# Second block's mixers: w_in in unsplit 32-bit matmuls, and split buffers in six tiles instead of three

## The chip, the cores and the metric

The kernel runs on one core of a Trainium2 chip. Its engines are named in the profile as PE (TensorE matmuls), PEld (TensorE weight loads), DVE (VectorE), ACT (ScalarE), POOL (GpSimd) and SP (SyncE, which here only issues DMAs). The metric is the device time of one launch in microseconds; the median of three runs before the change is 2834.43 us (2833.59 to 2838.01).

## The reference, cut to what matters

A first block of two layers (attention mixers, a dense feed-forward and a mixture of experts) is followed by a second block of two layers. The change lies in the second block. A token block is x of 256 x 1024; all arithmetic is float32.

```
for l in range(2):
    h = rmsnorm(x, norm_mix_g[l])
    proj = h @ w_in[l]                       # 1024 x 4896
    qa, ka, va, qd, kd, vd, beta, decay, z, gates = split(proj)
    y_attn = grid_attention(rope(qa), rope(ka), va) @ w_o_attn[l]
    qkv = silu(conv5(concat(qd, kd, vd)))
    o = bidir_gated_deltanet(l2norm(qd), l2norm(kd), vd, beta, g)
    y_dn = (rmsnorm(o) * silu(z)) @ w_o_dn[l]
    x = x + (sigmoid(gates0) * y_attn + sigmoid(gates1) * y_dn) @ w_out[l]
    h = rmsnorm(x, norm_ffn_g[l])
    u = conv3(h @ w_up[l])                   # 1024 x 5632
    x = x + (silu(u_gate) * u_val) @ w_down[l]   # 2816 x 1024
```

The delta rule is computed in chunks of 64 tokens, both directions, with a triangular inverse for each chunk and head.

## The kernel before, in words

**Split products.** A float32 matmul is computed as three faster ones. A weight tile of 1024 columns is split: ACT writes the rounded part `wh` (L152), DVE or POOL subtracts it from the raw weights and writes the rest `wl` (L154). The input is split in the same way into `xTh` and `xTl` (`make_xT`, L209 and L210). A product is then wh·xh + wl·xh + wh·xl: `mm3` (L177 to L179) where the input is the stationary operand and tokens are the output's rows, and `feat_group` (L370 to L372) where the weights are stationary and features are the output's rows.

**Weights.** All weight matrices stand in one list of jobs, in order of use; a job is at most one megabyte (128 x 2048 floats) and is loaded by one DMA on SP's queue (`_dma`, L137). In the second block a job goes to one of two buffers (tag raw, RAW = 2). Jobs are cut into pieces of at most 1024 columns (`subs`), split ahead of use into three pairs of buffers (HALF = 3; `_split`, `fill`). `w()` gives the next piece to the code that multiplies. In the second block's mixer `share` is 2: every second subtraction goes to POOL; behind a `tok_parts` with `tail`, the next four go to POOL too (TURN). A load may be issued when the buffer's earlier job is one that has come into use; on the chip it waits until the last reader of that buffer has finished.

**The second block's mixer** (`mix2`), in order of its code: z and the delta rule's small inputs (`zgate(0)`, 272 columns of w_in), two groups of 256 columns of the delta rule's inputs (`dnfeat` 2 and 3, each followed by a convolution on DVE, L1172), the attention's q, k, v (512 and 256 columns, `tok_group`), `zgate(1)`, four more `dnfeat`, eight gate groups of 256 columns into `m` and `G8`, then w_o_attn, w_o_dn and `out_proj` with w_out. The delta rule (`delta`) is a generator between them: decay factors (L1406 to L1465), gram matrices and the triangular inverse on DVE (`XP`, L1580 to L1607), the last part of the inverse on PE (L1663, L1669), then 16 steps of pairs (`pair`, L1708 to L1754). Its element-wise products qk and kd run on POOL (L1622), placed behind the last split on POOL (`s.gq`). After `out_proj`, `rms_h` normalises each half of the tokens (L1122 to L1132) and transposes it on PE. Tiles named kd, qk and xv belong to the delta rule; xTl is the second half of the split input.

**The order.** Within an engine instructions run in a fixed order. That order is not the code's: a planner with a cost for each instruction places them by priority, weight splits with a high one (PRIO), and may put matmuls of later groups between the small ones of the delta rule. `behind` forbids an instruction to be placed before another one; the last gate group and w_o_attn are kept behind the delta rule's last step in this way.

Of the kernel before, what the change touches and what calls it, by code (L numbers as in the profile page):

```python
# [11 lines left out]
F32 = mybir.dt.float32  # L12
F32R = mybir.dt.float32r
# [4 lines left out]
OP = mybir.AluOpType  # L18
# [3 lines left out]
S = 256  # L22
NT = 2
KD = D // 128
# [8 lines left out]
class Net:  # L33
    def __init__(s, ctx, tc, A):
        s.tc, s.nc, s.A = tc, tc.nc, A
        s.const = ctx.enter_context(tc.tile_pool(name="const", bufs=1))
        s.wa = ctx.enter_context(tc.tile_pool(name="wa", bufs=1))
        s.pm = ctx.enter_context(tc.tile_pool(name="psum", bufs=1, space=bass.MemoryType.PSUM))
        s.sc = ctx.enter_context(tc.tile_pool(name="sc", bufs=2))
        s.n_ps = 0  # L40
        s.wx = (0, 0)
        s.share, s.turn = 0, -9
        s.st, s.hs = [None, None], [None, None]
        s.epi = []
        s.pace = None
        s.jobs = []
        s.subs, s.subj = [], []
# [3 lines left out]
        s.n_dma = s.n_split = s.n_used = s.n_raw = 0  # L51

    @contextmanager
# [19 lines left out]
    BANKS = dict(mm=2, sd=3, at=2, ex=1)  # L73
    SHARE = 2
    TURN = 4
    PRIO = 3000
    AHEAD = (7, 11)

    def add_jobs(s, jobs):
        for ap, k, n, kind in jobs:  # L80
            j = len(s.jobs)
            s.jobs.append((ap, k, n))
            if kind == "f":
# [13 lines left out]
    def feats(s, w, c0, n):  # L97
        k = w.shape[0] // 128
        v = w.rearrange("(k p) n -> p k n", p=128)
        return [(v[:, :, c0:c0 + n], k, n, "f")]  # L100

    def rows(s, w, step):
# [17 lines left out]
    def _dma(s, j, c):  # L120

        ap, k, n = s.jobs[j]
        tag = s.more(j)
        if tag:
            key, bufs, pool = tag, 1, s.const if tag in ("OA", "Wc", "xTh", "xTl") else s.reg
        elif j >= s.edge_j or s.n_ring % (s.RAW + s.wx[0]) < s.RAW:
# [12 lines left out]
        return True  # L139

    def _split(s, i):
        k0, k, n0, n = s.subs[i]
        raw = s.jobs[s.subj[i]][:, k0:k0 + k, n0:n0 + n]
        r = []
        for tag in ("wh", "wl"):
            if i >= s.edge_i or i % (s.HALF + s.wx[1]) < s.HALF:
                w = s.wa.tile([128, 1024], F32R, tag=tag, name=tag, bufs=s.HALF)
            else:
                w = s.wb.tile([128, 1040], F32R, tag=tag, name=tag, bufs=s.wx[1])[:, 8:1032]
            r.append(w[:, :k * n].rearrange("p (k n) -> p k n", k=k))  # L150
        with s.tc.high_priority(offset=s.PRIO):
            s.nc.scalar.copy(r[0], raw)  # L152
            eng = s.nc.gpsimd if 0 <= i - s.turn < s.TURN or s.share and i % s.share == 0 else s.nc.vector
            x = eng.tensor_tensor(out=r[1], in0=raw, in1=r[0].bitcast(F32), op=OP.subtract)  # L154
            if eng is s.nc.gpsimd:
                s.psub = x
        s.subs[i] = (r[0], r[1], k, n)

    def fill(s, ahead):
        last = min(s.n_used, len(s.subs) - 1)  # L160
        while s.n_dma < len(s.jobs) and s._dma(s.n_dma, s.subj[last]):
            s.n_dma += 1
        ahead = min(s.n_used + ahead, max(s.n_used + s.HALF, s.edge_i), len(s.subs))
        while s.n_split < ahead and s.subj[s.n_split] < s.n_dma:
            s._split(s.n_split)
            s.n_split += 1

    def w(s):
        s.fill(s.HALF + s.wx[1])
        r = s.subs[s.n_used]  # L170
        s.subs[s.n_used] = None
        s.n_used += 1
        return r
# [138 lines left out]
    def tok_parts(s, n, K, xch, lead=0, tail=0, tags=("mm", "mm")):  # L312
# [4 lines left out]
        pend, base = [], 0  # L317

        def run(tt, bs):
            tsl = slice(tt * 128, tt * 128 + 128)  # L320
            ends = []
            for b0, h, l, k in pend:
                for kk in range(k):
                    c = b0 + kk
                    xh, xl = xch(c)
                    for b in bs:
                        ns = slice(b * 512, min(n, b * 512 + 512))
                        ends.append(s.mm3(pss[tt][b][:, :ns.stop - ns.start], xh[:, tsl], xl[:, tsl], h[:, kk, ns],
                                      l[:, kk, ns], c == 0, c == K - 1))
            return ends[-1]  # L330

        i = 0
        if tail:
            s.turn, k = s.n_used, 0
            while k < K:
                u = s.subs[s.turn]
                k += u[1] if len(u) == 4 and isinstance(u[1], int) else u[2]
                s.turn += 1
        while base < K:
# [3 lines left out]
            i += 1  # L343
            if i < lead or base > K - tail and base < K:
                continue
# [11 lines left out]
    def tok_group(s, n, K, xh, xl, lead=0):  # L357
        return [p for _, _, p in s.tok_parts(n, K, lambda c: (xh[:, c], xl[:, c]), lead)]

    def feat_group(s, ps, xh, xl):  # L360
        mm = s.nc.tensor.matmul
        b = 0
        while b < ps.shape[1]:
            h, l, k, n = s.w()
            for j in range(n // 128):
                o = ps[:, b, :]
                sl = slice(j * 128, j * 128 + 128)
                for kk in range(k):
                    with s.paced():
# [441 lines left out]
    def moe(s, i, j, pp):  # L811
# [96 lines left out]
        for tt in range(NT):  # L908
            for n in range(2):
                s.layernorm(tt, n, gb, lambda tt, n: s.rms_h(tt, n, gain))  # L910

# [201 lines left out]

    def rms_h(s, tt, n, gain):

# [14 lines left out]
        for n in range(2):  # L1130
            ns = slice(n * 512, n * 512 + 512)
            nc.vector.scalar_tensor_tensor(h[:, ns], x(n), r, gain[:, ns], op0=OP.mult, op1=OP.mult)  # L1132
            s.make_xT(tt, h, (n,))

# [5 lines left out]
    def jobs_mix2(s, l):  # L1140
# [52 lines left out]
    def mix2(s, l):  # L1193
        nc, A = s.nc, s.A
        s.share = s.SHARE
        xh, xl = s.xTh, s.xTl
        cw = s.vec_T(A["dn_conv_w_2"][l].rearrange("k (b p) -> (k b) p", p=128), 60, "cw")
# [26 lines left out]
        def dnfeat(g):  # L1224
            ps = s.fps()
            s.feat_group(ps, xh, xl)
            u = cT[g // 4][:, 2 * g % 8:2 * g % 8 + 2, :]
# [35 lines left out]
        for g in (0, 1, 4, 5):  # L1263
            dnfeat(g)
        s.gq = s.psub
        next(dn)
# [16 lines left out]
        mT = []  # L1283
        s.share = 0
        for g in range(4):
            gs = slice(2 * g, 2 * g + 2)
# [110 lines left out]
    def delta(s, l, cT, zb, sv, hg):  # L1397
# [459 lines left out]
def program(tc, A, out):  # L1857
    with ExitStack() as ctx:
# [19 lines left out]
        with s.region("two", 0, 0, "mm"):  # L1878
# [3 lines left out]
            gain = s.rms_gain("norm_mix_g_2", 1)  # L1882
            s.ffn2(0, lambda tt, n: s.rms_h(tt, n, gain))
            s.mix2(1)
# [17 lines left out]
```

## Time and profile before

| | us |
|---|---|
| median of three runs | 2834.43 |
| profiled execution | 2838.87 |
| its span, first to last instruction | 2837.1 |
| first block | 0 to about 1827 |
| second block, layer 0: mixer, w_out and norm, feed-forward | 1827 to 2095, 2095 to 2132, 2132 to 2325 |
| second block, layer 1: mixer, w_out and norm, feed-forward | 2325 to 2607, 2607 to 2644, 2644 to 2837 |

The stretches are read from where the matmuls of each weight matrix begin in the timeline. Matmul records overlap: each has a tail of some 0.16 us behind the time in which the next one starts, so a busy PE is not a full one. The mean granted clock of TensorE over the span is 0.963.

### The profile page before, as it was taken

The page shows a single profiled execution, that of the slowest core. Times are in us where ns is not written, and L with a number is a line of the kernel's source. Part 1 is how long each engine was busy: PE and PEld are TensorE (multiplying, and loading weights), DVE is VectorE, ACT ScalarE, POOL GpSimd, SP SyncE. Part 2 cuts the span into 40 slices and gives each one's busy share as a digit, 9 for nine tenths or more (in the row PEclk, how much of TensorE's full clock was granted, in tenths as well). Part 3 has the DMA queues.
Part 4 walks back from the last instruction along what each step waited for, and adds up shares of the span by engine and source line. Part 5 has one row for each costly group of instructions (what it writes and reads, how often), then busy time and mean ns, then how long its engine had stood idle before and what let it go on. Part 6 is the DMA issues. An engine that isn't in the chain of part 4 may idle for free. (4 is left out here: it accounts for less than half of the span.)

```text
span 2837.1 us, 42537 instructions
## 1 busy us (share of the span) xinstructions
PE 2664.6 (94%) x16177; PEld 2322.2 (82%) x16177; DVE 2194.8 (77%) x3347; ACT 1723.8 (61%) x2643; POOL 513.8 (18%) x427
## 2 busy tenths in 40 slices
PE   8999999899999999999999999788989989799899
PEld 7988998798787878778788777577779977688897
DVE  6576654657788989889888998789777858977784
ACT  5464543456477778787777777565645535564553
POOL 3235000132400000000000000166520016641100
PEclk9999999999999999999999999898899999889999
DMA  7336564544779999999999998533145543213454
GB/s 216 120 120 200 179 193 158 170 127 147 243 265 362 350 346 362 343 347 359 360 340 354 353 353 290 178 107 105 38 150 167 182 149 122 90 53 120 149 181 161
DMA packets 350097, 610.39 MB, mean 215 GB/s; under 512 B 13626, under 2 KB 175752, under 8 KB 349888
## 3 DMA queue, kind: packets, MB, share of 16 engines
q1 hardware_dynamic: 347120, 601.34, 61.8%
q0 software_dynamic: 2768, 6.28, 1.0%
q8 instruction: 129, 2.11, 0.3%
q14 instruction: 80, 0.66, 0.1%
HBM read 606.56 MB, written 1.05 MB: 214 GB/s over the span
## 5 line engine op out<-in xcount | busy, mean ns | idle before, releaser
L152 ACT CAST wh<-raw 128x1024 fp32r<-128x1024 f32 (+3 forms) x1154 | 1186.7, 1038 | 705.6 <-PE mm L371 189.5
L154 DVE TENSOR_TENSOR wl<-raw,wh 128x1024 fp32r<-128x1024 f32 (+3 forms) x1031 | 1246.1, 1226 | 398.7 <-ACT wh L152 379.3
L370 PE MATMUL mm<-xTh,wh 128*128 128x256 f32 x1632 | 472.1, 289 | 5.3 <-DVE cT L1172 2.9
L372 PE MATMUL mm<-xTh,wl 128*128 128x256 f32 x1632 | 470.9, 289 | 3.4 <-DVE wl L154 1.7
L371 PE MATMUL mm<-xTl,wh 128*128 128x256 f32 x1632 | 472.8, 290 | 0.0
L154 POOL TENSOR_TENSOR wl<-raw,wh 128x1024 fp32r<-128x1024 f32 (+3 forms) x123 | 293.4, 2390 | 908.4 <-ACT wh L152 872.9
L178 PE MATMUL mm<-wl,xg 128*128 128x512 f32 x896 | 355.1, 396 | 1.6
L177 PE MATMUL mm<-wh,xg 128*128 128x512 f32 x896 | 352.8, 396 | 0.0
L179 PE MATMUL mm<-wh,xg 128*128 128x512 f32 x896 | 351.5, 392 | 0.0
L370 PEld LDWEIGHTS mm<-xTh,wh 128*128 128x128 f32 x1632 | 316.1, 194 | 11.6 <-issue 3.8
L372 PEld LDWEIGHTS mm<-xTh,wl 128*128 128x128 f32 x1632 | 316.6, 194 | 7.3 <-DVE wl L154 2.3
L371 PEld LDWEIGHTS mm<-xTl,wh 128*128 128x128 f32 x1632 | 315.0, 193 | 1.0
L178 PEld LDWEIGHTS mm<-wl,xg 128*128 128x128 f32 x896 | 168.3, 188 | 43.2 <-DVE wl L154 7.7
L177 PEld LDWEIGHTS mm<-wh,xg 128*128 128x128 f32 x896 | 168.3, 188 | 36.7
L179 PEld LDWEIGHTS mm<-wh,xg 128*128 128x128 f32 x896 | 168.4, 188 | 36.4
L178 PE MATMUL sd<-wl,ac 128*128 128x512 f32 x448 | 175.7, 392 | 0.0
L642 POOL DMA_DIRECT2D gb<-in_ln_ffn_g_dram x2 | 1.1, 564 | 963.2 <-DMA raw<-in_expert_w_dram 962.9
L179 PE MATMUL sd<-wh,ac 128*128 128x512 f32 x448 | 175.6, 392 | 0.0
L177 PE MATMUL sd<-wh,ac 128*128 128x512 f32 x448 | 143.9, 394 | 0.0
L370 PE MATMUL ex<-xTh,wh 128*128 128x256 f32 x384 | 112.1, 292 | 4.7 <-DVE cT L1172 4.7
L372 PE MATMUL ex<-xTh,wl 128*128 128x256 f32 x384 | 111.4, 290 | 1.5 <-POOL wl L154 1.5
L371 PE MATMUL ex<-xTl,wh 128*128 128x256 f32 x384 | 112.0, 292 | 0.0
(581 smaller groups left out, 4939.1 us busy)
## 6 DMA issues: line engine op xcount, KB each, us to landing
raw<-in_expert_w_dram SPq DMA_DIRECT2D x336, 1024.0 KB, 5.7
raw<-in_w_in_dram SPq DMA_DIRECT2D x74, 1024.0 KB, 5.1
raw<-in_w_up_dram SPq DMA_DIRECT2D x44, 1024.0 KB, 5.0
raw<-in_dense_w_dram SPq DMA_DIRECT2D x33, 1024.0 KB, 5.2
raw<-in_w_down_dram SPq DMA_DIRECT2D x22, 1024.0 KB, 4.9
raw<-in_w_out_dram SPq DMA_DIRECT2D x16, 1024.0 KB, 5.0
raw<-in_w_branch_diff_dram SPq DMA_DIRECT2D x8, 1024.0 KB, 4.9
raw<-in_w_ple_gate_dram SPq DMA_DIRECT2D x8, 1024.0 KB, 5.0
```

Source lines behind the costliest of these rows:

```text
L152: s.nc.scalar.copy(r[0], raw)
L154: x = eng.tensor_tensor(out=r[1], in0=raw, in1=r[0].bitcast(F32), op=OP.subtract)
L177: mm(out, lhsT=lh, rhs=rh, start=start, stop=False)
L178: mm(out, lhsT=lh, rhs=rl, start=False, stop=False)
L179: return mm(out, lhsT=ll, rhs=rh, start=False, stop=stop)
L370: mm(o, lhsT=h[:, kk, sl], rhs=xh[:, kk, :], start=kk == 0, stop=False)
L371: mm(o, lhsT=h[:, kk, sl], rhs=xl[:, kk, :], start=False, stop=False)
L372: mm(o, lhsT=l[:, kk, sl], rhs=xh[:, kk, :], start=False, stop=kk == k - 1)
L642: s.nc.gpsimd.dma_start(gb[:, 0], row_bc(s.A[nm + "_g"], i * D, D))
```

## The change

The first item is that w_in of the second block is no longer split. Its jobs get the kind "w": one piece each, raw, no cast and no subtraction. The normalised input of the mixers is kept as one float32 tile `xf` in xTh's place (`make_xf`), and products with `l is None` are one matmul of float32 operands. `dnfeat` 2 and 3 multiply the two halves of the tokens apart. Raw jobs of w_in are held until their matmuls have read them; they may use xTl's tile as a third buffer (and in layer 1, for jobs 2 and 3, kd's tile as well).

The second is that a free pair of buffers is found by use, not by index (`_slot`), and from w_o_dn to the start of the next mixer the tiles kd, qk and xv serve as three more pairs, six in all (`s.ext`). The third is that no subtraction of the second block is on POOL: `share` is no longer set in `mix2`, TURN is gone (in the first block too), and the products on POOL no longer wait behind a split.

```diff
+    def unsplit(s, jobs):
+        return [(*j[:3], "w") for j in jobs]
...
+        if j >= s.edge_j:
+            def last(key, bufs):
+                use = s.held.setdefault(key, [])
+                return use[-bufs] if len(use) >= bufs else -1
+
+            key, bufs = min([("wa", s.RAW)] + [(t, 1) for t in s.alt.get(j, ()) if s.alt_on], key=lambda k: last(*k))
+            tag, pool = {"wa": ("raw", s.wa), "xTl": ("xTl", s.const)}.get(key) or (key, s.reg)
...
+    def _slot(s, i):
+        some = [("wa", s.HALF)]
+        if s.wx[1] and i < s.edge_i:
+            some.append(("wb", s.wx[1]))
+        for key, bufs in some + [(t, 1) for t in s.ext]:
+            use = s.busy.setdefault(key, [])
+            if len(use) < bufs or use[-bufs] < s.n_used:
+                use.append(i)
+                return key
...
+        if i in s.whole:
+            s.subs[i] = (raw, None, k, n)
+            return
...
-            eng = s.nc.gpsimd if 0 <= i - s.turn < s.TURN or s.share and i % s.share == 0 else s.nc.vector
-            x = eng.tensor_tensor(out=r[1], in0=raw, in1=r[0].bitcast(F32), op=OP.subtract)
+            eng = s.nc.gpsimd if s.share and i % s.share == 0 else s.nc.vector
+            eng.tensor_tensor(out=r[1], in0=raw, in1=r[0].bitcast(F32), op=OP.subtract)
...
+        if rl is None:
+            return mm(out, lhsT=lh, rhs=rh, start=start, stop=stop)
...
+    def make_xf(s, tt, src, g):
+        if tt == 0 and g == 0:
+            s.xf = s.const.tile([128, KD, S], F32, tag="xTh", name="xf")
+        pt = s.ps([128, 4, 128], "sd")
+        for c in range(4):
+            s.tr(pt[:, c, :], src[:, (4 * g + c) * 128:(4 * g + c + 1) * 128])
+        s.nc.scalar.copy(s.xf[:, 4 * g:4 * g + 4, tt * 128:tt * 128 + 128], pt)
...
+                if l is None:
+                    for t in (slice(0, 128), slice(128, 256)) if apart else (slice(0, 256),):
+                        for kk in range(k):
+                            mm(o[:, t], lhsT=h[:, kk, sl], rhs=xh[:, kk, t], start=kk == 0, stop=kk == k - 1)
...
+        J = s.unsplit(J)
+        for i in range(len(J)):
+            s.alt[len(s.jobs) + i] = ("xTl", "kd") if l and i in (2, 3) else ("xTl",)
...
-        s.share = s.SHARE
-        xh, xl = s.xTh, s.xTl
+        s.ext = ()
+        xh, xl, s.alt_on = s.xf, None, True
...
-        s.gq = s.psub
...
         s.share = 0
+        s.ext = ("kd", "qk", "xv")
...
+        s.alt_on = False
         gain = s.rms_gain("norm_ffn_g_2", l)
...
-        def PT(**k):
-            with s.behind(s.gq):
-                nc.gpsimd.tensor_tensor(**k)
+        PT = nc.gpsimd.tensor_tensor
```

## Rows read from the trace of the kernel before

**Rows 1.** the page: busy time (share of the span) and instructions

```profile
PE 2664.6 (94%) x16177; PEld 2322.2 (82%) x16177; DVE 2194.8 (77%) x3347; ACT 1723.8 (61%) x2643; POOL 513.8 (18%) x427
```

**Rows 2.** stretches: length, busy (records) of PE, PEld, DVE, ACT, POOL, clock, DMA

```profile
1827.00:2007.00 180.00, 157.69 (x1038) 141.00 (x1036) 164.31 (x308) 103.82 (x208) 111.77 (x99) 0.90 0.33 101
1882.00:2007.00 125.00, 107.38 (x718) 95.02 (x718) 121.68 (x214) 76.75 (x155) 83.48 (x80) 0.89 0.31 94
1958.00:2007.00 49.00, 45.02 (x328) 40.97 (x326) 48.00 (x84) 30.48 (x65) 23.60 (x19) 0.93 0.29 87
2007.00:2062.00 55.00, 51.14 (x421) 40.97 (x422) 35.56 (x119) 34.45 (x112) 25.44 (x42) 0.84 0.10 31
2062.00:2095.00 33.00, 31.22 (x268) 30.40 (x267) 28.59 (x56) 14.89 (x24) 5.77 (x3) 1.00 0.46 145
```

**Rows 3.** chain of waits, 1827 to 2095, shares by line

```profile
by line: issue 7.3%; DVE wl L154 6.5%; DVE cT L1172 3.6%; DVE XP L1580 3.5%; DVE XP L1606 3.4%; DVE Ma L1534 3.3%; PE sd L1732 2.8%; PE sd L1719 2.6%; DVE rs_t L189 2.5%; DVE rs_t L190 2.4%; ACT wh L152 2.2%; PE at L1741 2.1%; PE mm L177 2.
```

**Rows 4.** PE: timeline (start, length), chain piece, source line (ns min/median/max)

```profile
1838.34 0.28 PE L370 MATMUL ex<-xTh,wh 128*128 128x256 f32 x1
1838.70 0.28 PE L370 MATMUL ex<-xTh,wh 128*128 128x256 f32 x1
1888.37 1.45 PE L1512 MATMUL sd<-rg,tri 128*128 128x512 f32 x3
L1512 PE MATMUL sd<-rg,tri x16: 590/594/1062, 1885.9 to 2393.5; 128*128 128x512 f32 x16
2097.14 0.23 PE mm L177
```

**Rows 5.** records with xTl on PE (one per product) by stretch

```profile
1827.00:2095.00 268.00, 88.32 (x288) 0.90 0.30 92
2325.00:2607.00 282.00, 90.33 (x288) 0.87 0.29 91
```

**Rows 6.** those with the tile wl: PE, PEld, DVE, POOL

```profile
1827.00:2007.00 180.00, 83.30 (x265) 54.45 (x265) 22.40 (x19) 44.86 (x18) 0.90 0.33 101
2062.00:2095.00 33.00, 22.33 (x81) 15.20 (x80) 8.54 (x7) 4.82 (x2) 1.00 0.46 145
```

**Rows 7.** DVE timeline, a step alone and steps over a POOL split

```profile
1836.78 2.36 DVE L154 TENSOR_TENSOR wl<-raw,wh 128x1024 fp32r<-128x1024 f32 x1 [1.69 <-ACT wh L152]
1840.57 0.18 DVE L1415 TENSOR_SCALAR sp<-sp 128x32 f32<-128x32 f32 x1
1841.63 2.38 DVE L1419 TENSOR_SCALAR sp<-sp 128x32 f32<-128x32 f32 x1
1979.73 1.85 DVE L1606 TENSOR_TENSOR XP<-X,XP 128x512 f32<-128x512 f32 x1
```

**Rows 8.** chain piece in which PE waits for w_out's split

```profile
2110.26 1.05 ACT wh L152
```

**Rows 9.** norm behind w_out: POOL timeline, chain pieces, like steps

```profile
2116.71 6.98 POOL L154 TENSOR_TENSOR wl<-raw,wh 128x1024 fp32r<-128x1024 f32 x3 [0.24 <-DVE X L1556]
2116.81 2.31 DVE r_y L202
2119.45 1.97 DVE r_y L202
2121.44 2.81 DVE h L1132
L1132 DVE SCALAR_TENSOR_TENSOR h<-xt,r_y,g x16: 737/749/2796, 1824.6 to 2641.6; 128x512 f32<-128x512 f32 x16
```

**Rows 10.** start of layer 1's mixer: chain pieces, source line

```profile
2324.37 1.80 DVE r2v L1127
2326.66 0.61 DVE xTl L210
L1127 DVE SCALAR_TENSOR_TENSOR r2v<-r x8: 149/160/1865, 1822.3 to 2638.6; 128x1 f32<-128x1 f32 x8
```

**Rows 11.** loads of w_in, KB each, median us to landing

```profile
raw<-in_w_in_dram SPq DMA_DIRECT2D x17, 1024.0 KB, 5.0
```

More of the change, by code (lines that the diff above doesn't have):

```diff
@@ L41, in __init__ @@
         s.wx = (0, 0)
-        s.share, s.turn = 0, -9
+        s.share = 0
         s.st, s.hs = [None, None], [None, None]
@@ L46, in __init__ @@
         s.jobs = []
-        s.subs, s.subj = [], []
+        s.subs, s.subj, s.whole, s.alt, s.alt_on = [], [], set(), {}, False
         s.edge_j = s.edge_i = s.n_ring = 0
@@ L51, in __init__ @@
         s.n_dma = s.n_split = s.n_used = s.n_raw = 0
+        s.busy, s.ext = {}, ()
     @contextmanager
@@ L73 @@
     BANKS = dict(mm=2, sd=3, at=2, ex=1)
-    SHARE = 2
-    TURN = 4
     PRIO = 3000
@@ L82, in add_jobs @@
             s.jobs.append((ap, k, n))
-            if kind == "f":
+            if kind == "w":
+                s.whole.add(len(s.subs))
+                s.subs.append((0, k, 0, n))
+            elif kind == "f":
                 c = min(n, 1024 // k)
@@ L139, in _dma, with _split @@
         return True
-    def _split(s, i):
+    def _slot(s, i):
[7 more added lines that the diff above has]
+                return key
+    def _split(s, i, slot):
         k0, k, n0, n = s.subs[i]
         raw = s.jobs[s.subj[i]][:, k0:k0 + k, n0:n0 + n]
+        if i in s.whole:
+            s.subs[i] = (raw, None, k, n)
+            return
         r = []
[L145 to L149, printed above, removed]
+        if slot in ("wa", "wb"):
+            pool, bufs = (s.wa, s.HALF) if slot == "wa" else (s.wb, s.wx[1])
+            n8 = 8 if slot == "wb" else 0
+            ws = [pool.tile([128, 1024 + 2 * n8], F32R, tag=tag, name=tag, bufs=bufs)[:, n8:n8 + 1024]
+                  for tag in ("wh", "wl")]
+        elif slot == "xv":
+            ws = [s.reg.tile([128, 1024], F32R, tag=slot, name="ww", bufs=2) for _ in range(2)]
+        else:
+            w = (s.const if slot in ("OA", "Wc") else s.reg).tile([128, 2, 1024], F32R, tag=slot, name="ww")
+            ws = [w[:, 0], w[:, 1]]
+        for w in ws:
             r.append(w[:, :k * n].rearrange("p (k n) -> p k n", k=k))
@@ L162, in fill, with w @@
             s.n_dma += 1
-        ahead = min(s.n_used + ahead, max(s.n_used + s.HALF, s.edge_i), len(s.subs))
-        while s.n_split < ahead and s.subj[s.n_split] < s.n_dma:
-            s._split(s.n_split)
-            s.n_split += 1
[L168 to L173, printed above, removed]
+        while ahead and s.n_split < len(s.subs) and s.subj[s.n_split] < s.n_dma:
+            slot = s.n_split in s.whole or s._slot(s.n_split)
+            if slot is None:
+                break
+            s._split(s.n_split, slot)
+            s.n_split += 1
+    def w(s, n=1):
+        s.fill(1)
+        r = s.subs[s.n_used:s.n_used + n]
+        s.subs[s.n_used:s.n_used + n] = [None] * n
+        s.n_used += n
+        return r if n > 1 else r[0]
     def mm3(s, out, lh, ll, rh, rl, start, stop):
         mm = s.nc.tensor.matmul
+        if rl is None:
+            return mm(out, lhsT=lh, rhs=rh, start=start, stop=stop)
         mm(out, lhsT=lh, rhs=rh, start=start, stop=False)
@@ L327, in run @@
                         ns = slice(b * 512, min(n, b * 512 + 512))
-                        ends.append(s.mm3(pss[tt][b][:, :ns.stop - ns.start], xh[:, tsl], xl[:, tsl], h[:, kk, ns],
-                                      l[:, kk, ns], c == 0, c == K - 1))
+                        ends.append(s.mm3(pss[tt][b][:, :ns.stop - ns.start], xh[:, tsl], None if l is None else xl[:, tsl],
+                                          h[:, kk, ns], None if l is None else l[:, kk, ns], c == 0, c == K - 1))
             return ends[-1]
         i = 0
[L333 to L338, printed above, removed]
         while base < K:
@@ L343, in tok_parts @@
             i += 1
-            if i < lead or base > K - tail and base < K:
+            if base < K and (i < lead or base > K - tail):
                 continue
@@ L357, in tok_group, with feat_group @@
     def tok_group(s, n, K, xh, xl, lead=0):
-        return [p for _, _, p in s.tok_parts(n, K, lambda c: (xh[:, c], xl[:, c]), lead)]
-    def feat_group(s, ps, xh, xl):
+        return [p for _, _, p in s.tok_parts(n, K, lambda c: (xh[:, c], None if xl is None else xl[:, c]), lead)]
+    def feat_group(s, ps, xh, xl, apart=False):
         mm = s.nc.tensor.matmul
@@ L909, in moe @@
             for n in range(2):
-                s.layernorm(tt, n, gb, lambda tt, n: s.rms_h(tt, n, gain))
+                s.layernorm(tt, n, gb, lambda tt, n: s.rms_h(tt, n, gain, True))
     def moe_rest(s, j, xs):
@@ L1111, in diff_attn, with rms_h @@
         s.steps.append(s.last_tr)
-    def rms_h(s, tt, n, gain):
+    def rms_h(s, tt, n, gain, full=False):
         nc = s.nc
@@ L1132, in rms_h @@
             nc.vector.scalar_tensor_tensor(h[:, ns], x(n), r, gain[:, ns], op0=OP.mult, op1=OP.mult)
-            s.make_xT(tt, h, (n,))
+            if full:
+                s.make_xf(tt, h, n)
+            else:
+                s.make_xT(tt, h, (n,))
     def rms_gain(s, nm, l):
@@ L1225, in dnfeat @@
             ps = s.fps()
-            s.feat_group(ps, xh, xl)
+            s.feat_group(ps, xh, xl, g in (2, 3))
             u = cT[g // 4][:, 2 * g % 8:2 * g % 8 + 2, :]
@@ L1882, in program @@
             gain = s.rms_gain("norm_mix_g_2", 1)
-            s.ffn2(0, lambda tt, n: s.rms_h(tt, n, gain))
+            s.ffn2(0, lambda tt, n: s.rms_h(tt, n, gain, True))
             s.mix2(1)
```

8 lines of the change are left out of this document (4 added, 4 removed).

## The prediction, made before the result was known

> **What bounds the kernel now.** I read the page's busy table first: over the whole span PE is busy 94% and DVE 77% [rows 1], so the span alone says TensorE. Then the stages of the second block, by the busy time in stretches [rows 2]. There it differs: in the mixer of layer 0, from 1882 to 2007 us, DVE is busy 121.7 of 125 us and PE 107.4; from 1827 to 2007 PE is busy 157.7 of 180 us, and as a PE record carries a modelled tail, PE is emptier than that. From 2007 to 2062 (the delta rule's 16 steps) both have air: a chain of small steps. From 2062 to 2095 PE is full (31.2 of 33). Layer 1's mixer has the same 288 products and takes 282 us where layer 0's takes 268 [rows 5]. The chain of waits agrees [rows 3]: from 1827 to 2095 its largest named parts are DVE's; the split's subtraction (L154) alone is 6.5% of 268 = 17.4 us and its cast (ACT L152) 2.2% = 5.9 us. So in the mixers the weight split stands on the path, and the reader should see that DVE is the bound there and PE not quite.
>
> **The change, part by part.**
>
> *1. PE, added.* One product of w_in was three matmuls and becomes one 32-bit matmul. Three of 256 columns take 1838.70 - 1838.34 = 0.36 us; three of 512 take 3 x 0.23 = 0.69 [rows 4]. A 32-bit call is two records (the loop at L1512 makes 8 calls in two layers, and there are 16 records); three records of 512 columns fill 1.45 us, the last one 0.59, so one takes (1.45 - 0.59)/2 = 0.43, a call 0.86, and with 256 columns half, 0.43 [rows 4]. A layer has 288 products [rows 5]: by the code 240 of 256 columns, 32 of 272, 16 of 512. Added: 240 x 0.07 + 32 x 0.08 + 16 x 0.17 = 16.8 + 2.6 + 2.7 = 22.1 us a layer, 265/288 of it (20.3) before 2007. The two groups cut into halves of 128 columns I cost at no difference; if their shorter records ran at 0.12 instead of 0.11 it would be 32 x 4 x 0.01 = 1.3 us.
> The Trainium skill (FP8 and Floating Point Precision, "TensorE Precision Notes") says that true FP32 takes four passes through the array. If each cost what a split pass costs here, a product of 256 columns would be 4 x 0.12 = 0.48 against 0.36, and a layer would gain about 35 us on PE instead of 22. The trace shows two records of double length, and this measured 0.43 is what I sum with.
>
> *2. DVE, ACT and POOL, removed.* From 1827 to 2007 there are 19 subtractions on DVE, 22.4 us, and 18 on POOL, 44.9 us [rows 6]; all are of w_in and go, with their casts on ACT (1.05 us each). The ones on POOL cost DVE as well: DVE instructions that meet one are stretched to its end. A 128x32 TENSOR_SCALAR takes 0.18 us alone and 2.38 at 1841.63, over a POOL split [rows 7]. Going through the timeline, 14 DVE instructions between 1827 and 2007 are over 0.4 us longer than their like while a POOL split runs, first at 1836.78 and last at 1979.73 [rows 7], 22.5 us in all. So DVE gets back up to 22.4 + 22.5 = 44.9 us: with its idle time as it is, a lower end of 180 - 44.9 = 135 us. What is late next is PE: its 157.7 + 20.3 = 178 us is the upper end if its present busy time were all real work. It is not: 795 of its records there are w_in's (3 x 265) at 0.12 to 0.23, about 99 us, and the other 243 of the 1038 I put at the same 0.12, 29 us, together 128, new 148, which leaves about 32 idle at 180. Between 135 and 178 I take 164, nearer to PE's row, because PE would then be at 148/164 = 90%: -16 us a layer. The casts hide inside that.
> [...]
>
> *3. After the delta rule (2062 to 2095).* Only one gate group of w_in is left (+1.1 us on PE). POOL's two splits there (4.8 us) go to DVE (+2.4), and stretch DVE no more. PE is the bound; more split buffers let it wait less. -1 us, bounds +4 and -4. In layer 1 w_in's last group sits in one of the two ring buffers (in layer 0, by the rotation of three, in xTl's place), and now holds it until its matmuls are done, so the next load (at most the 5.0 us of a full megabyte [rows 11], and then a cast of 1.05 and a subtraction of 1.2 us) starts about a group, 7 us, later, and only one group of w_o_attn, 8 products of 0.36 us, covers it: +4 us once, 0 to +6.
>
> *4. w_out and the norm behind it.* Here PE waits for one cast of w_out, 1.05 us [rows 8], and its subtraction (22.4/19 = 1.2 us as in [rows 6]); six slots instead of three let these run earlier: -2 us (0 to -2.25). Then, with PE waiting, the norm's DVE steps meet three POOL splits of w_up (6.98 us): 2.31, 1.97 and 2.81 us against 0.16, 0.16 (what a step on one column takes [rows 10]) and 0.75 alone [rows 9], 6.0 us lost on the path. These splits now go to DVE at 1.2 us each, at worst all in the same place: 3.6. Between -6 and -2.4 I take -3.
>
> *5. Start of a mixer.* The transposed input is one copy instead of cast and subtraction; the subtraction (0.61 us [rows 10]) goes, and so does the POOL split that made a 128x1 step take 1.80 us there [rows 10] (median 0.16). -2 us (0 to -3). The loads: unsplit buffers are held until the matmuls end, three of them in rotation; a megabyte takes 5.0 us [rows 11] and a group on PE 16 x 0.43 = 6.9, so the load of the group after next is hidden; if only two rotated, each group would show up to 5.0 us.
>
> *6. First block.* A few splits behind its out-projections move from POOL to DVE as well; the same trade as in 4, three places, 0 (-3 to +3). w_up and w_down are bound by PE; six slots do nothing for them.
>
> Sum: a layer -16 - 1 - 2 - 3 - 2 = -24; two layers -48, +4 for layer 1: **-44 us**. The profiled execution took 2838.87 us around its span of 2837.1; the median of the runs is 2834.43. From that median: **2790 us**.
>
> **Rivals.**
>
> *A. DVE is all of it.* The stage falls to about 154 instead of 164, with gates moved into the delta rule's gaps. For: DVE's 121.7 of 125. Against: PE would need 148/154 = 96% of the stage. 10 us more in each layer: 2770.
>
> *B. PE takes the bound.* The mixer up to 2007 stays at about 178 and only parts 3 to 6 remain: 2 x (-2 - 8) + 4 = -16: 2818. For: 157.7 + 20.3. Against: the tails in that number.
>
> *C. Slower: gates pushed behind the delta rule.* PE takes its work in a planned order, and w_in's gates fill its gaps. Where the chain shortens and a group needs 6.9 us instead of 5.8, the plan may place groups after the delta rule, where PE is full and each stands on the path for 6.9 us. One does now, by order. The gain of 24 a layer is gone from the fourth further group on (27.6); with five it is +10.5 a layer, +4: 2834 + 25 = 2859. For: PE is busy 45.0 of 49 from 1958 to 2007 [rows 2]. Against: the delta rule's stretch has gaps, and a group can be cut into 0.2 us records.
>
> *D. It nets out.* Half of A to C's mechanisms at once, within 0.2% (5.7 us, about what a measurement can tell from no change): 2829 to 2840.
>
> **How the numbers follow.** Forecast (2780 to 2805) 0.48; A 0.15; B 0.19; D 0.06; C 0.12. Faster by over 0.2% holds the forecast, A and B: 0.82. Same 0.06, slower 0.12. The range 2762 to 2836 leaves out C (0.12), some of D and the end of A; the forecast's own is 2780 to 2805.
>
> **What would show it.** Right: in the mixers no L152 or L154 on w_in and no POOL split; w_in's matmuls as two records of 0.21 us a call; the 128x32 steps all at 0.18; the stretch from the first transposes to the end of the gates about 164 us; the norm after w_out some 3 us shorter; the chain of waits shows more PE and no L154 before the delta rule. Wrong: DVE's small steps stay stretched over POOL's multiplies; PE waits for DMA in the mixer; two or more gate groups after the delta rule; or the sum of the mixers is what it was with PE full (B).

## The result, and the profile after

The changed kernel takes 2800.70 us (four runs, 2799.07 to 2802.48) beside 2836.22 for the kernel before on the same chip: a ratio of 0.9877, 95% interval 0.9863 to 0.9892, or 35.5 us less. The forecast was 2790 us, 44 less. The profiled execution has a span of 2798.9 us, 38.2 less than before.

Stages, from the first PE record of each in the timeline (us; layer 0, layer 1):

| stage | before | after | difference |
|---|---|---|---|
| first block, to the mixer's first transpose | 1825.5 | 1828.0 | +2.5 |
| to the last part of the inverse on PE | 181.4, 186.1 | 165.8, 169.0 | -15.6, -17.1 |
| from there to the delta rule's first step | 21.7, 29.6 | 27.0, 27.0 | +5.4, -2.6 |
| from there to w_out | 66.1, 67.5 | 64.5, 67.2 | -1.6, -0.3 |
| w_out, to the first transpose of the norm | 29.6, 29.6 | 27.2, 28.8 | -2.4, -0.8 |
| rest of the norm | 7.4, 7.4 | 6.2, 6.6 | -1.2, -0.8 |
| w_up | 126.6, 126.7 | 126.9, 126.9 | +0.3, +0.2 |
| w_down, to the next mixer or the end | 65.0, 66.9 | 62.6, 65.3 | -2.4, -1.6 |

First the page of the changed kernel, busy time, beside [rows 1]: PE has 7.4 us more (not the 2 x 22.1 that term 1 adds; why is told below), DVE 113 us less, POOL 174 us less.

```profile
PE 2672.0 (95%) x15729; PEld 2296.6 (82%) x15729; DVE 2081.7 (74%) x3320; ACT 1646.1 (59%) x2559; POOL 340.1 (12%) x362
```

Next the stretches of layer 0's mixer in the changed kernel, columns as in [rows 2].

```profile
1828.00:1994.00 166.00, 159.34 (x790) 125.85 (x790) 116.01 (x292) 73.18 (x179) 59.79 (x85) 0.94 0.33 103
1994.00:2021.00 27.00, 27.00 (x169) 24.40 (x169) 9.73 (x33) 12.02 (x33) 4.16 (x6) 1.00 0.26 78
2021.00:2058.00 37.00, 33.64 (x331) 24.51 (x331) 26.93 (x86) 20.38 (x74) 12.85 (x31) 1.00 0.15 46
2058.00:2085.00 27.00, 27.00 (x214) 26.59 (x214) 23.14 (x53) 12.63 (x19) 0.67 (x1) 1.00 0.41 137
```

In [rows 2] DVE was the engine without air up to 2007 us; now PE is busy 159.3 of 166 us and DVE 116.0. The chain of waits of the changed kernel from 1829 to 2085 us, by line, says the same: where [rows 3] began with L154's subtraction, it now begins with w_in's own matmuls (L409, L211), and no subtraction of a weight is among its named parts.

```profile
by line: PE mm L409 12.3%; PE mm L211 7.4%; DVE cT L1222 4.9%; DVE Ma L1585 4.1%; PE ex L409 3.8%; DVE XP L1657 3.7%; PE sd L1781 2.8%; PE ex L211 2.7%; DMA raw<-in_w_o_attn_dram 2.6%; issue 2.5%; PE at L1790 2.3%; POOL qa L1376 2.2%; DVE X
```

A stage average hides what matters here, so the mixer's first part is cut further: stretches of the kernel before, and then the same of the changed kernel.

```profile
1828.00:1874.00 46.00, 42.21 (x263) 38.47 (x262) 33.63 (x71) 21.27 (x42) 22.64 (x16) 0.90 0.37 117
1874.00:1899.00 25.00, 21.75 (x137) 17.55 (x136) 24.82 (x55) 14.90 (x32) 17.48 (x14) 0.93 0.40 126
1899.00:1965.00 66.00, 54.72 (x365) 49.75 (x366) 63.87 (x111) 38.22 (x74) 51.17 (x54) 0.87 0.33 98
```

```profile
1828.00:1874.00 46.00, 46.00 (x248) 35.67 (x249) 21.77 (x72) 11.99 (x32) 7.26 (x10) 0.96 0.37 117
1874.00:1899.00 25.00, 24.61 (x123) 18.78 (x121) 19.10 (x52) 12.90 (x30) 20.72 (x26) 1.00 0.42 130
1899.00:1965.00 66.00, 62.06 (x288) 49.99 (x286) 63.95 (x139) 28.70 (x67) 19.88 (x34) 0.92 0.32 96
1965.00:2021.00 56.00, 53.67 (x306) 45.81 (x305) 20.92 (x64) 31.60 (x85) 16.09 (x21) 0.94 0.25 76
```

From 1899 to 1965 us (gram matrices, inverse, convolutions) DVE is full in both kernels; in the changed one it gets through 139 records there instead of 111, and PE is busy 62.06 of the 66 us. Before 1874 and behind 1965 PE is full and DVE has room. By busy time the mixer has two full engines in turn, not one; what either is worth these rows do not say.

Two more things changed. The first is where w_in's products stand. Their records (the tile xTl, one a product, before; xf, two a product, after) up to the inverse, layer 0 and layer 1, before and then after (length, busy time and records of PE, clock, DMA):

```profile
1827.00:2007.00 180.00, 81.47 (x265) 0.90 0.33 101
2325.00:2509.40 184.40, 77.60 (x249) 0.87 0.33 104
...
1828.00:1994.00 166.00, 122.79 (x534) 0.94 0.33 103
2309.00:2477.00 168.00, 122.21 (x534) 0.95 0.32 100
```

534 records are 235 products (the 32 products cut into halves have four records each). So 30 products in layer 0 and 14 in layer 1, 12.9 and 6.0 us at 0.43, left this stage for the stretches behind it.

The second is the granted clock of TensorE, the column behind the five engines in the stretches. Up to the inverse it rose from 0.90 to 0.94, behind it from 0.84 (2007 to 2062) to 1.00, over the span from 0.963 to 0.978. The clock has two levels, 2.4 GHz (1.00 in the column) and 1.2 GHz (0.50); at the lower one three passes of 256 columns take 1999.00 - 1998.36 = 0.64 us, against 0.36 in [rows 4]. In the kernel before:

```profile
1998.00:2000.00 2.00, 2.00 (x10) 2.00 (x10) 1.97 (x3) 1.93 (x8) 1.92 (x2) 0.50 0.00 0
...
1998.36 0.41 PE L370 MATMUL mm<-xTh,wh 128*128 128x256 f32 x1
1999.00 0.41 PE L370 MATMUL mm<-xTh,wh 128*128 128x256 f32 x1
```

Added up over the second block, PE is busy at the lower level for 126.6 us before and 52.4 us after. By the two prices (and 0.43 against 0.22 us from start to start of w_in's 32-bit records of 256 columns) 32 to 37 us of PE time came back in this way, an estimate; that is most of the difference between the 44.2 us of term 1 and the page's 7.4. PE's idle time up to the inverse fell along with it, from 22.3 of 180 us to 6.7 of 166. No run holds the clock fixed, so what the change would give without it, and whether the smaller gaps raised the clock, is not shown.

### The profile page after: what moved, and what is told of

Its sections match the earlier page's. It is cut to its first block, busy times and chain, and to the rows that moved or that the text cites. A ratio compares the mean times of both kernels' runs of the same rounds, so it can differ in the third digit from the quotient of the medians.

```text
span 2798.9 us, 41249 instructions
## 1 busy us (share of the span) xinstructions
PE 2672.0 (95%) x15729; PEld 2296.6 (82%) x15729; DVE 2081.7 (74%) x3320; ACT 1646.1 (59%) x2559; POOL 340.1 (12%) x362
## 5 line engine op out<-in xcount | busy, mean ns | idle before, releaser
L187 DVE TENSOR_TENSOR wl<-raw,wh 128x1024 fp32r<-128x1024 f32 (+1 forms) x938 | 1131.5, 1225 | 329.7 <-ACT wh L185 309.9
L185 ACT CAST wh<-raw 128x1024 fp32r<-128x1024 f32 (+1 forms) x996 | 1028.4, 1043 | 571.8 <-PE mm L214 163.2
L414 PE MATMUL mm<-xTh,wh 128*128 128x256 f32 x1096 | 313.7, 286 | 1.4 <-ACT cqn L552 1.4
L415 PE MATMUL mm<-xTl,wh 128*128 128x256 f32 x1096 | 314.4, 287 | 0.0
L416 PE MATMUL mm<-xTh,wl 128*128 128x256 f32 x1096 | 311.0, 284 | 0.2 <-DVE wl L187 0.2
L414 PEld LDWEIGHTS mm<-xTh,wh 128*128 128x128 f32 x1096 | 209.1, 191 | 3.7 <-ACT cqn L552 1.7
L416 PEld LDWEIGHTS mm<-xTh,wl 128*128 128x128 f32 x1096 | 209.3, 191 | 0.6 <-DVE wl L187 0.4
L187 POOL TENSOR_TENSOR wl<-raw,wh 128x1024 fp32r<-128x1024 f32 x58 | 143.0, 2466 | 334.5 <-ACT wh L185 324.9
L409 PE MATMUL mm<-xf,raw 128*128 128x256 f32 (+1 forms) x704 | 150.5, 365 | 0.0
L409 PEld LDWEIGHTS mm<-xf,raw 128*128 128x128 f32 x704 | 120.2, 196 | 17.6 <-issue 3.7
```

Of the source, the lines that this page charges most:

```text
L409: mm(o[:, t], lhsT=h[:, kk, sl], rhs=xh[:, kk, t], start=kk == 0, stop=kk == k - 1)
L414: mm(o, lhsT=h[:, kk, sl], rhs=xh[:, kk, :], start=kk == 0, stop=False)
L415: mm(o, lhsT=h[:, kk, sl], rhs=xl[:, kk, :], start=False, stop=False)
L416: mm(o, lhsT=l[:, kk, sl], rhs=xh[:, kk, :], start=False, stop=kk == k - 1)
```

## The experiments

All were made from one of the two kernels; the kernel before ran beside each group, with medians of 2833.67 (first four), 2834.46 (next four) and 2835.59 us (last four). The changed kernel's 2800.70 stood beside 2836.22, so a difference to it of some 2.5 us says nothing. The mean granted clock of the profiled executions is 0.963 in experiments 1 and 2, as before, 0.971 in 3, 0.960 in 6, 0.980 in 10 and 0.976 to 0.980 in the others: the times hold its share too.

**1. The kernel before, all subtractions on DVE.**

```diff
-    SHARE = 2
-    TURN = 4
+    SHARE = 0
+    TURN = 0
```

> The kernel before with every subtraction on DVE (SHARE = 0, TURN = 0); w_in is still split, three pairs of buffers. My theory (the gain of the change is DVE's time, its own splits and the stretch under POOL's splits together): in a mixer DVE loses 18 x 1.2 = 21.6 us to the splits that come over from POOL and gets back the 22.5 us of stretch, so the stage up to the inverse stays within 3 us of 180; only the norm behind w_out and the mixer's start gain, some 3 to 4 us a layer: 2836 to 2828. Rival 'the blocked port is all of it': the stage gains as in the changed kernel, 15 us a layer: about 2805. Third: 1.2 us of DVE costs more than the stretch did: 2845.

Measured: 2824.11 us, ratio 0.9962 (0.9949 to 0.9975). It is 10 us below before and 4 us below the lower end of my range (2836 to 2828): the stage up to the inverse is 175.8 and 175.3 us, 5.6 and 10.8 less, not within 3. From the delta rule to w_out it gives 9.0 and 3.4 us back. And the chain of waits of this kernel from 1829 to 2000 us shows at what price:

```profile
by line: DVE wl L154 20.2%; issue 8.7%; DVE cT L1172 6.5%; DVE Ma L1534 6.1%; DVE XP L1606 4.9%; PE ex L372 3.1%; PE ex L371 2.4%; PE ex L370 2.4%; PE mm L370 2.3%; PE mm L371 2.1%; PE mm L372 2.0%; DVE rs_y L191 1.9%; PE sd L214 1.8%; DVE 
```

The subtraction is now 20.2% of 171 us, 35 us, of the path. Norm and w_out give 3.8 us a layer, with three pairs of buffers.

**2. The changed kernel with w_in split.**

```diff
-        J = s.unsplit(J)
...
-        xh, xl, s.alt_on = s.xf, None, True
+        xh, xl = s.xTh, s.xTl
...
```

> The changed kernel with w_in split again, all on DVE, and the six pairs of buffers kept (what is undone is the first item alone). My theory: as in the kernel before with all subtractions on DVE, and some 2 us a layer less for the w_out stage: about 2825; so the unsplit products are worth about 25 us of the 35. Rival 'the buffers are most of it': about 2805 here. Rival 'the blocked port is all of it': about 2803.

Measured: 2822.73 us, 0.9958 (0.9946 to 0.9971): as forecast, the same as experiment 1 within their spread. So the unsplit products are worth 22 us, with what the clock gives back (0.963 here, 0.978 there); most of the rest is what experiment 1 gains by moving POOL's subtractions, 10 us. The mixers (first transpose to w_out) are 273.5 and 270.6 us here, 257.3 and 263.2 in the changed kernel.

**3. Idle subtractions on POOL in the changed kernel.**

```diff
             s.subs[i] = (raw, None, k, n)
+            f = s.jobs[s.subj[i]].rearrange("p k n -> p (k n)")
+            if k * n == 2048:
+                x = s.wa.tile([128, 1024], F32R, tag="wl", ...)
+                with s.tc.high_priority(offset=s.PRIO):
+                    s.nc.gpsimd.tensor_tensor(out=x, in0=f[:, :1024], in1=f[:, 1024:], op=OP.subtract)
```

> The changed kernel and, for each w_in job of 2048 columns, one subtraction of 128x1024 on POOL at the splits' priority, whose result nobody reads (about as many as POOL had before). My theory: DVE is stretched again by about 20 us in a mixer, but it is at 116 of 166 us there and PE is the bound, so about a quarter of it lands: +5 us a layer, 2810. Rival 'the blocked port is all of it': +15 a layer, 2831. Rival 'PE is the bound and nothing else counts': 2801.

Measured: 2846.91 us, 1.0048 (1.0036 to 1.006): 46 us above the changed kernel, and slower than before. My 2810 is refuted; "the port is all of it", at 2831, is nearer and still too low. What the subtractions do to DVE shows in this kernel's DVE timeline, one POOL row, and its group of the 16 products into Ma; the last line of the second fence is the same group in the changed kernel.

```profile
1845.43 3.50 DVE L1477 SCALAR_TENSOR_TENSOR sp<-sp,sp 128x32 f32<-128x32 f32 x6
1848.96 2.38 DVE L1478 SCALAR_TENSOR_TENSOR sp<-sp,sp 128x32 f32<-128x32 f32 x1
...
1848.95 2.35 POOL L174 TENSOR_TENSOR idle<-raw 128x1024 fp32r<-128x1024 f32 x1 [0.75 <-DMA raw<-in_w_in_dram]
...
L1590 DVE TENSOR_TENSOR Ma<-kk,Ma 64x256 f32<-64x256 f32 x16 | 19.4, 1248 | 0.6 <-ACT kk L1583 0.5
```

```profile
1844.28 1.32 DVE L1472 SCALAR_TENSOR_TENSOR sp<-sp,sp 128x32 f32<-128x32 f32 x6
1845.63 0.19 DVE L1473 SCALAR_TENSOR_TENSOR sp<-sp,sp 128x32 f32<-128x32 f32 x1
...
L1585 DVE TENSOR_TENSOR Ma<-kk,Ma 64x256 f32<-64x256 f32 x16 | 13.1, 857 | 0.4 <-ACT kk L1578 0.2
```

A step of 0.19 us takes 2.38 when it meets a POOL subtraction. Added up over the DVE records that overlap one and are over 0.4 us longer than the shortest of their kind: 27.4 us (15 records) and 23.1 us (14) in the two mixers, 50.5 together. The time rose by 46.2, but up to the inverse, where these records stand, only by 16.9 and 10.1; 13.9 us lie behind the inverse of layer 1. PE, busy only 45.3 of the 66 us from 1899 to 1965, waits for DVE there. POOL's own queue is not the cause in layer 0: in this kernel's chain of waits from 1828 to 2042 us no POOL piece is among the 130 longest, where the changed kernel has `qa` at 2.2%. The stretch and the chain:

```profile
1899.00:1965.00 66.00, 45.34 (x203) 36.37 (x203) 62.88 (x95) 25.39 (x59) 43.07 (x52) 0.86 0.26 82
...
by line: PE mm L216 12.5%; PE mm L414 11.1%; DVE Ma L1590 7.5%; DVE cT L1227 5.4%; PE ex L216 4.9%; DMA raw<-in_w_o_attn_dram 4.8%; DVE XP L1636 4.4%; DVE XP L1662 4.4%; ACT Md L1604 2.8%; PE sd L254 2.3%; issue 2.2%; DVE XP L1639 1.7%; PE 
```

**4. The same subtractions on DVE.** The edit is that of 3 with `s.nc.vector`.

> The changed kernel and, for each w_in job of 2048 columns, one subtraction of 128x1024 on DVE (1.2 us each, 16 or so a layer, 20 us), whose result nobody reads. My theory: DVE rises from 116 to about 136 of 166 us, PE stays the bound, a quarter lands: +5 us a layer, 2810. Rival 'DVE's time counts one for one': +20 a layer, 2840. Rival 'PE is the bound and nothing else counts': 2801.

Measured: 2805.03 us, 0.9897 (0.9883 to 0.9911): 4.3 us more for 45.3 us of work (34 subtractions), between my 2810 and the rival's 2801. DVE's time is cheap where nobody waits for the result: of 17 subtractions in layer 0 the trace has five, 6.1 us, between 1899 and 1965.

**5. Memsets on POOL in their place.**

```diff
+                    for e in (1024, 1024, 512):
+                        s.nc.gpsimd.memset(x[:, :e], 0.0)
```

> The changed kernel and, for each w_in job of 2048 columns, three memsets on POOL (1024, 1024 and 512 columns, about 2.4 us together by the 0.95 us of the one of 1024 columns) at the splits' priority in the place of the idle subtraction that cost 46 us. Theory now: what cost 46 us there is that DVE's steps are stretched over a POOL subtraction (24 us in the mixer of layer 0, 21 in layer 1), and they land because DVE is the bound between 1899 and 1965 us; a memset reads nothing, DVE should not be stretched: 2801 to 2806. Rival 'POOL's queue': its own products (qa, kd, qk) come late behind the idle work: 2835 to 2847.

Measured: 2808.8 us, 0.9911 (0.9897 to 0.9924), 8 us above the changed kernel and above my 2801 to 2806. How much of the 8 us is the memsets' is open: three of the six runs take 2802.77 to 2807.16 us at a clock of 0.980, three, the profiled one among them, 2810.44 to 2814.71 at 0.975 to 0.977. The test is also weaker than meant: memsets wait for no load, so in layer 0 they ran in one bunch at the mixer's start (31 records from 1823.45 to 1846.93 us, 19 before it), not where the subtractions had stood, and POOL's queue as a rival is hardly tested. But some DVE steps are stretched, against what I expected: DVE's timeline before and under that bunch.

```profile
1828.09 1.41 DVE L1181 SCALAR_TENSOR_TENSOR h<-xt,r_y,g 128x512 f32<-128x512 f32 x2
...
1842.17 4.80 DVE L1468 TENSOR_SCALAR sp<-sp 128x32 f32<-128x32 f32 x1
1842.25 4.74 DVE L1463 TENSOR_SCALAR gb<-gb 128x32 f32<-128x32 f32 x1
1847.00 0.19 DVE L1469 TENSOR_TENSOR sp<-sp,sp 128x32 f32<-128x32 f32 x1
```

A TENSOR_SCALAR of 0.17 us takes 4.80, until the memsets end, in layer 1 6.50 (at 2327.38); `h`, a step with two inputs from SBUF, takes its usual 0.75 under them (two overlapping ones 1.41). The two steps together are stretched by 11.0 us.

**6. Half of PE's w_in work.**

```diff
-                        for kk in range(k):
+                        for kk in range(0, k, 2):
...
```

> The changed kernel with 136 of the 288 products of w_in in a layer left out (every second one of a feature group, three of eight of a token group): about 61 us less on PE a layer. Theory now: PE is full from 1828 to 1874 and from 1965 to 2021, DVE bounds what lies between; so about 102 of 193 us gain, 61 x 102/193 = 32 a layer: about 2737. Rival 'PE bounds the whole mixer': 61 a layer, 2680. Rival 'the chain is one of small steps, PE is only filled up with w_in': under 10 a layer, over 2780.

Measured: 2741.33 us in the one run (forecast 2737), 59 us less for 122 us of PE work. The number came, the reason did not. Up to the inverse 91 of the 235 products of a layer are left out, some 42 us, and this stage falls by 39.1 and 42.6 us: there nearly all of it lands. Behind the inverse 45 more are left out (19 us), and yet the stretch to w_out is 13.3 and 6.0 us longer, at a granted clock of 0.80 and 0.89 where the changed kernel has 1.00. Layer 0 up to the inverse and from there to w_out:

```profile
1831.00:1957.70 126.70, 105.65 (x536) 82.51 (x536) 112.32 (x268) 62.85 (x152) 62.80 (x82) 0.92 0.50 156
1957.70:2062.40 104.70, 91.74 (x661) 78.07 (x662) 70.90 (x199) 54.13 (x152) 20.66 (x40) 0.80 0.16 52
```

**7 to 9. Some gate groups split again** (N = 3, 6, 8 of the last ones).

```diff
-        J = s.unsplit(J)
+        J = s.unsplit(J[:-N]) + J[-N:]
...
+                if g + 4 * (dst is G8) == 8 - N:
+                    xh = s.const.tile([128, KD, S], F32R, tag="xTl", name="xh2")
+                    xl = [s.wa.tile([128, 4, S], F32R, tag=t, name="xl2", bufs=1) for t in ("wh2", "wl2")]
+                    for c in (0, 4):
+                        nc.scalar.copy(xh[:, c:c + 4], s.xf[:, c:c + 4])
+                        nc.vector.tensor_tensor(out=xl[c // 4], in0=s.xf[:, c:c + 4], in1=xh[:, c:c + 4].bitcast(F32), op=OP.subtract)
```

> The changed kernel with the last three gate groups (of 256 columns) of w_in split again: xf is cast and subtracted once before them, xh in xTl's place and xl in one of the three pairs of buffers. PE is full from 1965 to 2021 us and DVE is busy 21 of these 56 us there, so the 6 subtractions and the 2 of xf have room. Theory: PE saves 3 x 16 x 0.07 = 3.4 us a layer, and raw buffers come free at the cast: -3 a layer, 2795. Rival 'their subtractions, at high priority, run early and stand in DVE's full stretch before 1965': +7 a layer, 2815. Rival 'nets out': 2801.

> The same with the last six gate groups split. Theory: PE saves 6.7 us a layer, but xf's conversion and some of the 12 subtractions (1.2 us each) now fall before 1965, where DVE is full: between -4 and +4 a layer, 2793 to 2809, and above gates3. Rival 'PE alone counts': -6.7 a layer, 2787, below gates3.

> As gates6, with all eight gate groups split, so that the conversion of xf comes behind the last group that feeds the delta rule. Theory: PE saves 8.8 us a layer and nearly all of the 16 subtractions stand where DVE has room: 4 us a layer below the changed kernel for gates6, 5 here: 2790. Rival 'PE has nothing to fill its gaps with before the conversion is done': over 2800.

Measured: N = 3: 2800.43 us, 0.9880 (0.9866 to 0.9895). N = 6: 2792.9, 0.9855 (0.9841 to 0.9869). N = 8: 2799.61, 0.9877 (0.9861 to 0.9892). With three groups my 2795 did not come, but "nets out" (2801). The stretch between the inverse and the delta rule falls from 27.0 to 20.9 and 19.2 us, but the stage before it grows by 3.2 and 3.4 us, and w_o_attn and w_o_dn give back 4.8 and 7.0. Why they do I can only argue: one of three pairs of buffers holds xl until the last gate, and a load of w_out stands on the chain from 1994 to 2085 us:

```profile
by line: PE mm L415 7.8%; PE mm L414 7.6%; PE mm L416 7.5%; PE sd L1790 7.0%; DMA raw<-in_w_out_dram 5.9%; PE at L1799 5.6%; PE sd L1777 5.2%; DVE wl L187 4.7%; PE sd L1721 3.8%; PE sd L1727 3.5%; PE ex L416 3.4%; PE ex L414 3.4%; DVE xv L1
```

With six the forecast's first end holds, and the order of 3 and 6 is the rival's. Its four runs (2791.66 to 2794.38) all lie below every run of the changed kernel, and below those of N = 3 beside it, though the intervals of the ratios overlap by 0.0003 to 0.0006. With eight my 2790 did not come; PE has less to fill its gaps with before xf is converted, which was the rival there (over 2800). The stretches of N = 6 and then of N = 8 (PE 58.0 against 54.0):

```profile
1899.00:1965.00 66.00, 57.95 (x279) 47.03 (x279) 62.50 (x140) 33.91 (x74) 23.07 (x39) 0.92 0.23 67
1965.00:2021.00 56.00, 53.33 (x401) 49.54 (x399) 40.51 (x81) 41.18 (x93) 19.28 (x21) 0.94 0.31 102
```

```profile
1899.00:1965.00 66.00, 53.99 (x296) 46.51 (x295) 64.73 (x140) 33.55 (x67) 17.37 (x28) 0.87 0.22 72
```

**10. The kernel before with POOL's subtractions of the second block left out.**

```diff
+            if eng is s.nc.gpsimd and i >= s.edge_i:
+                r[1] = r[0]
+            else:
```

> The kernel before with the second block's subtractions on POOL left out (the low part of these pieces is then the high part again; casts and the three matmuls of a product stay, and DVE's own subtractions). It shows what POOL's subtractions cost where w_in is split. Theory now (what lands is DVE's work in the stretch from about 1900 to 1965 where it is full, stretches included): 18 subtractions fewer than in the kernel with all of them on DVE, of which about two fifths stood in that stretch, 8.6 us a layer: 2824 - 17 = 2807. Rival 'DVE's own 1.2 us hardly count' (as the idle ones in the changed kernel: 2 us a layer): 2820. Rival 'only the port counts, and POOL's splits were all of the 35 us': 2800 or less.

Measured: 2759.13 us, 0.9733 (0.972 to 0.9746), 76.5 us less, far below my 2807 and the first rival's 2820; of the three only "the port", with 2800 or less, holds. The kernel before has 43 DVE records over 0.4 us longer than their like over a POOL split in the second block (14 of them those of term 2, [rows 7]); their excess is 35.0 us in layer 0 and 39.3 in layer 1, 74.3 together. The two sums are alike, but that a stretched microsecond costs one does not follow: PE is busy at the lower clock for 48.9 us of the second block here, against 126.6 before, so 34 to 39 of the 76.5 us may have come through the clock (an estimate as above). PE's waits for POOL's own results are not it: 1.5 us up to the inverse of layer 0 in the kernel before. Doing these subtractions on DVE (experiment 1) gives 65 of the 76.5 back.

**11 and 12. Two raw buffers; three pairs.**

```diff
-            s.alt[len(s.jobs) + i] = ("xTl", "kd") if l and i in (2, 3) else ("xTl",)
+            s.alt[len(s.jobs) + i] = ()
```

```diff
-        s.ext = ("kd", "qk", "xv")
+        s.ext = ()
```

> The changed kernel with w_in's raw jobs in the two ring buffers alone (no third one in xTl's or kd's place). Theory: a load takes 5 us and a group of 16 products on PE 6.9, so two buffers nearly hide it: 2801 to 2806. Rival 'the raw ring is a bound': up to 5 us for each of 18 jobs, 2840 and more.

> The changed kernel with three pairs of buffers for the split weights everywhere (s.ext always empty), so without the second item. Theory: the w_out stage waits for a cast again, 2 us a layer: 2805. Rival 'buffers are most of the gain': 2820 or more. Rival 'they do nothing': 2801.

Measured: 2801.55 us, 0.9877 (0.9862 to 0.9892), and 2801.51 us, 0.9880 (0.9865 to 0.9895): neither the third raw buffer nor the six pairs show in the time; of the second run's three expectations "they do nothing" came, not my 2805. In the traces the six pairs are worth 1.6 us of each w_down (64.2 and 66.9 us without) and nothing in w_out (27.6 and 28.4).

## Why the prediction was right, and where not

*The bound.* The reading held: splits on the path in the mixer, PE "not quite". What it missed is that, by busy time, the stage has two full engines in turn; experiment 6 does not give their shares. It also took PE's busy time beyond 128 us for tails, pricing every record at the upper clock, although [rows 2] show 0.90 for this stage: by (1 - 0.90) x 2 some 36 of the 180 us are at the lower level. What the change gives back through the clock is in no term. The sum came within its range in part by luck: the clock, and products that left the stage, stood in for what the terms lacked.

*1, PE added.* The price of a product is as summed; the sum itself shows neither in the stage (30 and 14 products left it) nor in the page (the clock). In the changed kernel's timeline eight records of 512 columns take 3.60 us, of which 0.16 is tail, so 0.43 each as in [rows 4], and in its chain 48 records of 128 columns take 0.112 each, so the cut groups cost next to nothing.

```profile
1854.92 3.60 PE L211 MATMUL mm<-raw,xf 128*128 128x512 f32 x8
...
1841.46 5.36 PE ex L409 x48
```

*2, splits removed.* -16 a layer forecast, -15.6 and -17.1 measured: the size came, the reason held by half. I had let 265 products stay before the inverse, and 235 do; up to the delta rule's first step the layers gain 10.2 and 19.7 us. I added DVE's own subtractions (22.4 us) and the stretch under POOL's (22.5) as one stock of DVE time, capped by PE. Two runs show the stretch to be dear: 76.5 us of time for 74.3 of stretch (10), 46.2 for 50.5 (3), the clock's share in both. DVE's own cost a tenth of their length where nobody waits for them (4.3 us for 45, experiment 4) and all of it where PE does (65 us of time for the 56 x 1.2 = 67 us that moved over in experiment 1, with the clock back at 0.963). From experiment 10's kernel to the changed one the stage grows by 14.0 and 13.8 us, with 235 products in it instead of 260 and 252, each product dearer on PE, and 19 subtractions fewer on DVE; -30 and +14 make the -16. Why a stretch is dearer than a subtraction that nobody waits for I can only argue: the planner knows the one and puts it where there is room; it doesn't know the other, which strikes whichever step runs.

*3, after the delta rule.* From the delta rule to w_out -1.6 and -0.3 for the forecast -1. The +4 of layer 1 did not come: from w_o_attn's first product to w_o_dn's it went from 15.2 to 13.9 us. What came instead is +5.4 us before the delta rule in layer 0 (and -2.6 in layer 1), which I had in no term: rival C's mechanism, one step earlier than I put it. Gates fill that stretch until PE is busy 27.00 of 27.00 us. The chain goes there through two loads of w_o_attn, held behind raw w_in jobs:

```profile
2011.84 3.40 DMA raw<-in_w_o_attn_dram
...
2017.59 3.26 DMA raw<-in_w_o_attn_dram
```

PE was full beside them, and with two raw buffers the stretch is 24.5 us, so these loads are not shown to be the cause.

*4, w_out and the norm.* -5 a layer forecast, -3.6 and -1.6 measured; this term of the sum was mis-sized by half. The -2 for w_out came in layer 0 (-2.4) and not in layer 1 (-0.8), and not from the six slots (12: nothing): it comes from the first subtractions of w_up and w_out being off POOL (1: -2.0 with three pairs). PE still waits for w_out's split, as in [rows 8], and w_up's subtractions now stand between the norm's steps, which are as short as [rows 9] let one hope (0.68 instead of 2.81). The chain of the changed kernel:

```profile
2104.75 1.06 ACT wh L185
2105.83 1.23 DVE wl L187
...
2109.25 1.23 DVE wl L187
2110.55 0.31 DVE ww L187
...
2111.75 0.68 DVE h L1176
```

*5, the mixer's start.* The subtraction and the stretched step of [rows 10] are gone, but the first products ran beside them: they lie in the stage of term 2 and can't be told apart from it. "w_down: nothing" was wrong by 1.6 us a layer (12).

*6, the first block.* +2.5 measured. The changed kernel and the ten made from it, whose first block does the same work, have it at 1825.2 to 1831.3 us, so this is not told from 0.

*The rivals.* A did not come: DVE's share does not stand alone. B is half true: PE is the bound at both ends of the mixer, but the stage is 166 and 169 us, not 178. D did not come. C shows as the products that left the stage and as the +5.4. The sum of the layers is -17.6 and -23.0, against -24 and -20.

One of the prediction's signs of being wrong did show in part: the 128x32 steps are short again (0.19 us in the fences of experiment 3), but other DVE steps stay stretched over POOL's multiplies. By the measure of experiment 3 these are 30 steps and 26.7 us in the two mixers of the changed kernel. In layer 1, for instance, two steps of a group whose mean is 0.86 us in layer 0 take 5.29 between them, over a row of multiplies; no run shows what these cost in time.

```profile
2390.52 5.29 DVE L1585 TENSOR_TENSOR Ma<-kk,Ma 64x256 f32<-64x256 f32 x2
...
2393.44 2.95 POOL L1676 TENSOR_TENSOR qk<-qk,msk 128x256 f32<-128x256 f32 x4
```

## What to carry to other kernels

Price an engine that blocks another by the stretched steps in the trace, and do it before counting its busy time: 28 subtractions a layer, on an engine that the page has at 18%, cost 38 us a layer. No one price holds for a stretched microsecond: up to the inverse of layer 0 it came to 1.3 us of time in experiment 10 (29.6 for 22.5) and 0.6 in experiment 3 (16.9 for 27.4). Read the granted clock beside PE's busy time, before the change and after: here it moved with PE's gaps and changed PE's busy time by nearly as much as the change itself added. Count how much work stands in a stage before comparing its length. Cut a stage until each piece has one full engine; a change that trades DVE for PE can pay in one piece and cost in the next, and the version with the lowest time (2792.9 us, six gate groups split) saves PE work where PE is full. Move a piece of work and leave it out in two separate runs: the first shows what the trade brings, the second what the work costs.

## What the runs showed of the hardware

Which DVE steps are blocked depends on what POOL does. Over a POOL subtraction, which reads two tiles and writes one, steps with two inputs from SBUF are stretched (0.19 to 2.38 us), but also TENSOR_SCALAR ([rows 7], 0.18 to 2.38) and copies (128x10, 0.17 to 2.27 us at 1890.62 in experiment 3). Over memsets a 128x32 TENSOR_SCALAR waits (0.17 to 4.80 us), while `h` keeps its 0.75 us. The convolution's steps, with one input from PSUM, stay at 0.48 us over a subtraction.

The Trainium skill (SBUF — State Buffer, "Who interferes with whom") has this: two-input steps contend with a GpSimd instruction that reads, not with one that only writes, while copies and tensor_scalar may enter a two-port mode that contends. The traces agree in each case named. The TENSOR_SCALAR of [rows 7] reads a single tile and is stretched all the same (0.18 to 2.38 us): the exception for the two-port modes belongs to the rule, and counting inputs is not enough.

Not settled: how much of the gain is the clock's, why w_o_attn in layer 1 takes 20 us instead of 13.9 in experiments 3 and 4, and which of the changed order's parts makes the 5.4 us before the delta rule.
